# A 90-degree rotation on one core: stores on their own queue, issued when nearly all loads have landed

## Chip, cores, metric

One core of a Trainium2 chip. The metric is device time in microseconds (us), the median over executions. VectorE, ScalarE and SyncE are engines of the core; SBUF and PSUM are its on-chip memories; DMA engines move data between SBUF and the chip's main memory.

## The reference

```python
def setup_inputs():
    return {"x": np.random.randn(32, 3, 256, 256).astype(np.float32)}

def reference(x):
    return np.rot90(x, k=-1, axes=(-2, -1)).astype(np.float32)
```

25.17 MB go in and 25.17 MB come out. No arithmetic is done: data is loaded, transposed on VectorE in 32 x 32 blocks, and stored.

## The kernel before

The tensor is cut into 12 units of 2 MB, all of which fit into SBUF at once. Unit n is transposed into the buffer of unit n - 1, and the first unit into PSUM (`turned0`), from where ScalarE copies it at the end. No buffer has to be waited for, so the loads can run at full rate, and the stores follow in the same queue, SyncE's. A transfer of 1 MB is 128 packets of 8 KB (64 of 16 KB for most loads), and 16 DMA engines report its end.

```python
    for n in range(n_slabs):
        if n == last:
            nc.sync.dma_start(out=units[n], in_=ld8_v[n])          # 2 MB, 8 KB rows
            continue
        for i in range(I):
            if n == 0:
                nc.sync.dma_start(out=units[n][:, i], in_=ld8_v[n][:, i])
            else:                                                  # 1 MB, 16 KB rows
                nc.sync.dma_start(out=units[n][i::I].rearrange("p i f -> p (i f)"), in_=ld16_v[n, i])
    for n in range(n_slabs):
        t_in, t_out = units[n], units[n - 1] if n else turned0
        # ... two nc.vector.transpose from t_in to t_out (cut) ...
        if n == 1:
            nc.sync.dma_start(out=st_v[n][:, 0, :W], in_=t_out[:, 0, :W])   # 128 KB
            nc.sync.dma_start(out=st_v[n][:, 0, W:], in_=t_out[:, 0, W:])   # 896 KB
            nc.sync.dma_start(out=st_v[n][:, 1], in_=t_out[:, 1])           # 1 MB
        elif n:
            nc.sync.dma_start(out=st_v[n], in_=t_out)                       # 2 MB
    for i in range(I):
        nc.scalar.copy(out=units[last][:, i], in_=turned0[:, i])
    nc.sync.dma_start(out=st_v[0], in_=units[last])
```

Of the kernel before, what the change touches and what calls it, by code (L numbers as in the profile page):

```python
# [1 line left out]

# [4 lines left out]




@with_exitstack
def kernel(
    ctx: ExitStack,
    tc: tile.TileContext,
    x: bass.AP,
    out: bass.AP,
):

















    nc = tc.nc
    fp32 = mybir.dt.float32

    B, C, H, W = x.shape
    P = nc.NUM_PARTITIONS  # L40
    RI, RO = 16, 8
    K = H // RI
    I = 2
    Q = P // (K * I)
    n_slabs = B * C // (Q * I)
    last = n_slabs - 1
    F = RO * W

    rows_in = x.rearrange("b c h w -> (b c h) w")
    rows_out = out.rearrange("b c h w -> (b c h) w")  # L50
    ld8_v = rows_in.rearrange("(n i p r) w -> n p i (r w)", i=I, p=P, r=RO)
    ld16_v = rows_in.rearrange("(n i m r) w -> n i m (r w)", i=I, m=Q * K, r=RI)
    st_v = rows_out.rearrange("(n i p c) w -> n p i (c w)", i=I, p=P, c=RO)

    pools = [ctx.enter_context(tc.tile_pool(name=f"unit{u}", bufs=1)) for u in range(n_slabs)]
    units = [pool.tile([P, I, F], fp32, name=f"u{u}") for u, pool in enumerate(pools)]
    psum = ctx.enter_context(tc.tile_pool(name="psum", bufs=1, space=bass.MemoryType.PSUM))
    turned0 = psum.tile([P, I, F], fp32, name="turned0")

    for n in range(n_slabs):  # L60
        if n == last:
            nc.sync.dma_start(out=units[n], in_=ld8_v[n])
            continue
        for i in range(I):
            if n == 0:
                nc.sync.dma_start(out=units[n][:, i], in_=ld8_v[n][:, i])  # L66
            else:
                nc.sync.dma_start(out=units[n][i::I].rearrange("p i f -> p (i f)"), in_=ld16_v[n, i])

    for n in range(n_slabs):  # L70
        t_in, t_out = units[n], units[n - 1] if n else turned0
        if n in (0, last):
            for i in range(I):
                src = t_in[:, i].rearrange("p (r g c) -> p c r g", r=RO, c=RO)
                dst = t_out[:, i].rearrange("p (c g r) -> p c r g", c=RO, r=RO)
                nc.vector.transpose(out=dst[:, :, ::-1, ::-1], in_=src)  # L76
        else:
            src = t_in.rearrange("p i f -> p (i f)").rearrange("p (r g c) -> p c r g", r=RI, c=RO)
            dst = t_out.rearrange("p i (c k r) -> p c r k i", c=RO, r=RI)[:, :, ::-1, ::-1, :]
            for h in range(2):  # L80
                cs = slice(h * RO // 2, (h + 1) * RO // 2)
                nc.vector.transpose(out=dst[:, cs], in_=src[:, cs])  # L82

        if n == 1:
            nc.sync.dma_start(out=st_v[n][:, 0, :W], in_=t_out[:, 0, :W])
            nc.sync.dma_start(out=st_v[n][:, 0, W:], in_=t_out[:, 0, W:])
            nc.sync.dma_start(out=st_v[n][:, 1], in_=t_out[:, 1])
        elif n:
            nc.sync.dma_start(out=st_v[n], in_=t_out)  # L89

    for i in range(I):
        nc.scalar.copy(out=units[last][:, i], in_=turned0[:, i])  # L92
    nc.sync.dma_start(out=st_v[0], in_=units[last])


# [1 line left out]
_INS = ['x']  # L97
_OUTS = [((32, 3, 256, 256), 'float32')]


# [23 lines left out]
```

## Time and profile before

| | before |
|---|---|
| time | 124.06 us (3 runs) |
| span of the profile | 122.2 us |
| bytes over the span | 50.33 MB, 412 GB/s |
| rate inside loads and inside stores | 429 GB/s |
| "the turn" (last loads, first stores) | 59 to 63 us |

In the views below, a "stretch" line reads: start and end in us, length, busy time of VectorE, ScalarE and GpSimd, clock share, busy share of the DMA engines, GB/s. In a DMA view, the 40 numbers after `GB/s` are equal slices of the stretch asked for. Some statements rest on single packets: the trace records start and duration of each packet that a DMA engine moved, and of the 4-byte packet with which each of the 16 engines reports the end of a transfer. I call the time from the first to the last of these 16 reports of one transfer the *spread* of the engines. A transfer has landed when its semaphore, which counts these reports, is seen complete. Each profile is of one execution.

### The profile page before, as it was taken

The numbers are of one execution on the slowest core, as the hardware profiler recorded it, in microseconds if no ns is written. First come the engines' busy times: TensorE is split into PE (matmuls) and PEld (weight loads), VectorE is DVE, ScalarE is ACT, GpSimd is POOL, SyncE is SP. The second block draws the span as 40 slices with busy tenths as digits, with TensorE's granted clock in tenths as the row PEclk, the third lists the DMA queues.
The fourth block names the chain that finished last, engine by engine and source line by source line (L and its number), as shares of the span: only waits on it lengthen the run. The fifth ranks groups of instructions, "written<-read, shape, count | busy, mean of one in ns | idle before, by whom it ended". The sixth has DMA issues, their size and how long they took to land.

```text
span 122.2 us, 134 instructions
## 1 busy us (share of the span) xinstructions
DVE 93.3 (76%) x24; ACT 5.0 (4%) x3; POOL 0.2 (0%) x4
## 2 busy tenths in 40 slices
DVE  0299999999999999999999999999999940000000
ACT  0000000000000000000040000000000651000000
POOL 0000000000000000000000000000000000000000
DMA  3999999999999999999999999999999999999993
GB/s 88 429 432 434 440 440 429 429 429 429 429 429 429 429 429 424 434 424 408 370 414 428 426 429 429 429 429 429 429 429 429 424 429 429 429 429 426 429 429 166
DMA packets 5584, 50.33 MB, mean 412 GB/s; under 512 B 592, under 2 KB 720, under 8 KB 848
## 3 DMA queue, kind: packets, MB, share of 16 engines
q1 hardware_dynamic: 5584, 50.33, 97.8%
HBM read 25.17 MB, written 25.17 MB: 412 GB/s over the span
## 4 chain that ended last, share of the span: by engine, by line
DMA 57%; DVE 13%; issue 7%; DVEq 3%; ACT 2%; SPq 1%
DMA u<-in_x_dram 39%; DMA out_dram<-u 18%; DVE u L82 10%; DVE u L76 3%; DVEq L119 3%; ACT u L92 2%; SPq L66 1%; SPq L89 0%
## 5 line engine op out<-in xcount | busy, mean ns | idle before, releaser
L82 DVE STREAM_TRANSPOSE u<-u 128x2048 f32<-128x2048 f32 x20 | 78.0, 3948 | 0.3
L76 DVE STREAM_TRANSPOSE turned<-u 128x2048 f32<-128x2048 f32 x2 | 7.6, 3828 | 5.5 <-DMA u<-in_x_dram 5.5
L76 DVE STREAM_TRANSPOSE u<-u 128x2048 f32<-128x2048 f32 x2 | 7.8, 3953 | 0.0
L92 ACT COPY u<-turned 128x2048 f32<-128x2048 f32 x2 | 3.7, 1866 | 33.8 <-DVE u L76 33.8
L92 ACT ACT_TABLE_LOAD x1 | 1.3, 1283 | 62.4 <-DMA u<-in_x_dram 62.4
L108 POOL MEMSET const-bfloat16-1.0<- 128x1 bf16 x1 | 0.1, 102 | 0.0
L108 POOL MEMSET const-uint8-127<- 128x1 uint8 x1 | 0.1, 102 | 0.0
L108 POOL MEMSET const-float32-0.0<- 128x1 f32 x1 | 0.1, 99 | 0.2 <-issue 0.2
L108 POOL MEMSET const-float32-1.0<- 128x1 f32 x1 | 0.1, 99 | 0.0
## 6 DMA issues: line engine op xcount, KB each, us to landing
u<-in_x_dram SPq DMA_DIRECT2D x22, 1024.0 KB, 19.6
out_dram<-u SPq DMA_DIRECT2D x11, 2048.0 KB, 25.0
u<-in_x_dram SPq DMA_DIRECT2D x1, 2048.0 KB, 22.5
out_dram<-u SPq DMA_DIRECT2D x1, 1024.0 KB, 20.2
out_dram<-u SPq DMA_DIRECT2D x1, 896.0 KB, 20.2
out_dram<-u SPq DMA_DIRECT2D x1, 128.0 KB, 20.6
```

Source lines behind the costliest of these rows:

```text
L66: nc.sync.dma_start(out=units[n][:, i], in_=ld8_v[n][:, i])
L76: nc.vector.transpose(out=dst[:, :, ::-1, ::-1], in_=src)
L82: nc.vector.transpose(out=dst[:, cs], in_=src[:, cs])
L92: nc.scalar.copy(out=units[last][:, i], in_=turned0[:, i])
L108: nc = _bacc.Bacc("TRN2", target_bir_lowering=False, num_devices=1)
L119: with _tile.TileContext(nc) as tc:
```

## The change

The intent: keep loads and stores apart, each in a queue of its own, with transfers of mostly 1 MB. The first store waits until the first quarter of the last 1 MB has landed; the other three quarters are to cover the time that the store takes to start.

```diff
+    stores = []
+    def store(dst, src, after=None, cls=mybir.DependencyClass.NoSync):
+        st = nc.scalar.dma_start(out=dst, in_=src)
+        after = after or stores[-1]
+        tc.add_manual_dep(st.ins, after.ins.name, mybir.DependencyInfo(
+            cls, mybir.DependencyReason.SCHED_ONLY), reason="order of transfers")
+        stores.append(st)
     for n in range(n_slabs):
-        if n == last:
-            nc.sync.dma_start(out=units[n], in_=ld8_v[n])
-            continue
         for i in range(I):
-            if n == 0:
+            if n == last and i == 1:
+                parts = [slice(0, P, 4), slice(2, P, 4), slice(1, P, 2)]
+                lds = [nc.sync.dma_start(out=units[n][ps, i], in_=ld8_v[n][ps, i]) for ps in parts]
+            elif n in (0, last):
                 nc.sync.dma_start(out=units[n][:, i], in_=ld8_v[n][:, i])
         # ... cut ...
         if n == 1:
+            store(st_v[n][:, 0, :W], t_out[:, 0, :W], lds[0], mybir.DependencyClass.Sync)
+            store(st_v[n][:, 0, W:], t_out[:, 0, W:])
+            store(st_v[n][:, 1], t_out[:, 1])
+        elif n > last - 3:
+            store(st_v[n], t_out)
         elif n:
-            nc.sync.dma_start(out=st_v[n], in_=t_out)
+            for i in range(I):
+                store(st_v[n][:, i], t_out[:, i])
         # ... cut: the last 2 MB too are stored in two halves
```

More of the change, by code (lines that the diff above doesn't have):

```diff
@@ L84 @@
         if n == 1:
-            nc.sync.dma_start(out=st_v[n][:, 0, :W], in_=t_out[:, 0, :W])
-            nc.sync.dma_start(out=st_v[n][:, 0, W:], in_=t_out[:, 0, W:])
-            nc.sync.dma_start(out=st_v[n][:, 1], in_=t_out[:, 1])
+            store(st_v[n][:, 0, :W], t_out[:, 0, :W], lds[0], mybir.DependencyClass.Sync)
[3 more added lines that the diff above has]
+            store(st_v[n], t_out)
         elif n:
-            nc.sync.dma_start(out=st_v[n], in_=t_out)
+            for i in range(I):
+                store(st_v[n][:, i], t_out[:, i])
     for i in range(I):
         nc.scalar.copy(out=units[last][:, i], in_=turned0[:, i])
-    nc.sync.dma_start(out=st_v[0], in_=units[last])
+    for i in range(I):
+        store(st_v[0][:, i], units[last][:, i])
 _INS = ['x']
```

## The prediction

> **What bounds the kernel now.** I read the page first: busy table, slices, queue line, DMA issues. One queue carries everything, and the 16 DMA engines are busy for nearly the whole span.
>
> ```profile
> DVE 93.3 (76%) x24; ACT 5.0 (4%) x3; POOL 0.2 (0%) x4
> DMA  3999999999999999999999999999999999999993
> GB/s 88 429 432 434 440 440 429 429 429 429 429 429 429 429 429 424 434 424 408 370 414 428 426 429 429 429 429 429 429 429 429 424 429 429 429 429 426 429 429 166
> q1 hardware_dynamic: 5584, 50.33, 97.8%
> HBM read 25.17 MB, written 25.17 MB: 412 GB/s over the span
> ```
>
> The reader is to see three things. VectorE, at 76%, is not the bound. The rate stands at 429 GB/s in loads (first half) and in stores (second half) alike, so a store costs what a load costs. And there are only three places where the rate falls: the start, the slices 18 to 21 in the middle (408, 370, 414), and the end. 50.33 MB at 429 GB/s is 117.3 us of a span of 122.2 us; the whole change has 4.9 us to work on, and most of that is start and end.
>
> So I sized the three places. First the stretch where loads end and stores begin, as the table of chosen stretches has it (time, DVE, ACT, POOL, clock, DMA share, GB/s):
>
> ```profile
> 8.00:56.00 48.00, 47.79 (x13) 0.00 (x0) 0.00 (x0) 1.00 1.01 429
> 56.00:59.00 3.00, 3.00 (x2) 0.00 (x0) 0.00 (x0) 1.00 0.98 410
> 59.00:61.00 2.00, 1.97 (x2) 0.00 (x0) 0.00 (x0) 1.00 0.96 328
> 61.00:63.00 2.00, 2.00 (x1) 0.64 (x1) 0.00 (x0) 1.00 1.02 416
> 66.00:118.00 52.00, 33.09 (x9) 3.73 (x2) 0.00 (x0) 1.00 1.01 428
> ```
>
> Against 429 GB/s the turn loses 2.0 x (1 - 328/429) = 0.47 us, 3.0 x (1 - 410/429) = 0.13 us and 2.0 x (1 - 416/429) = 0.06 us: 0.66 us in all, with the engines still shown busy (0.96 to 1.02). They are not starved of work; packets take longer. The packet records say the same: 8 KB packets take 309 ns nearly everywhere, but 440 to 775 ns for the last few load packets of each engine between 59.3 and 60.8 us. By the packets that post each engine's share of a semaphore, the earliest engine loses 0.30 us there and the latest about 0.7 us, so the engines come out 0.6 us apart and stay so to the end.
>
> Then the start and the end, from the DMA view cut to 4 us (40 slices of 0.1 us):
>
> ```profile
> GB/s 0 0 0 0 0 0 0 0 0 0 0 0 0 0 0 0 0 410 246 0 164 0 0 0 492 164 0 573 328 246 573 410 328 492 492 328 492 492 328 492
> GB/s 246 573 410 328 573 410 328 573 410 328 492 410 328 492 492 246 410 655 246 246 246 328 82 164 0 0 0 0 0 0 0 0 0 0 0 0 0 0 0 0
> ```
>
> The first line is 0 to 4 us: data starts at 1.7 us and is at full rate from 2.4 us. The second is 118.2 to 122.2 us: the rate thins over the last 0.6 us (the engines that come in apart) and the last packet starts at about 120.5 us. Neither the first loads nor the last 2 MB are changed in kind.
>
> Last, who could be late for a store. The timeline:
>
> ```profile
> 0.73 0.86 SPq L66 DMA_DIRECT2D u<-in_x_dram  x2
> 42.28 0.36 SPq L85 DMA_DIRECT2D out_dram<-u  x1
> 49.60 50.02 SPq L89 DMA_DIRECT2D out_dram<-u  x10
> 91.47 7.75 DVE L76 STREAM_TRANSPOSE u<-u 128x2048 f32<-128x2048 f32 x2
> 99.26 1.87 ACT L92 COPY u<-turned 128x2048 f32<-128x2048 f32 x1 [1.93 <-DVE u L76]
> 101.15 0.37 SPq L93 DMA_DIRECT2D out_dram<-u  x1
> DMA to landing us min/median/max: 17.0/25.4/29.9
> ```
>
> The first store is issued at 42.28 us, 19 us before its turn: it stands in the ring behind the loads, so there is no gap at the turn. The last store is issued at 101.15 us and the last line (the view of the store line in the loop, L89) says that a store waits at least 17 us in the ring before it lands. VectorE's end at 99.2 us therefore has more than 10 us of slack.
>
> **What the Trainium skill says.** "DMA: Bandwidth & Descriptors", section "Issuing engines are not separate DMA queues", says that transfers started on different engines run on the same 16 DMA engines and interleave, and that issuing on several saves sequencer time alone. The trace before has one queue, so it can't show the interleaving, but issuing is not what it waits for. Same page, "Where 436 GB/s comes from": the fabric ceiling is 435 GB/s; the trace has 429, 98.6% of it, in both directions, so no faster stores are to be hoped for. Same page, "Latency and other measured facts": about 600 ns to the first byte for transfers issued from SyncE or ScalarE. The trace has about 1.0 us from the start of the first issue (0.73) to the first data (1.7), of which 0.39 us is the issuing instruction; I use 1.0 us. Same page, "Queues, rings and completion order": a DMA engine with work in two queues takes turns between them packet by packet, and a semaphore increment comes after that engine's earlier writes. In the trace the last store's semaphore packet ends at 120.83 us and it counts as landed at 121.18 us; over all transfers that step is 0.3 to 0.6 us, median 0.42 us.
>
> **The change part by part.**
>
> Stores move to ScalarE, their order pinned. Alone, this could let them run from 20 us on, among the loads; the wait on the first forbids it. Bytes are unchanged: 117.3 us stays.
>
> The last 1 MB load becomes 256 KB + 256 KB + 512 KB, every fourth partition, every fourth offset by two, every second. Each still spreads over the 16 engines (2, 2 and 4 packets of 8 KB on each), so an engine still has 8 x 306 ns = 2.45 us of work in it.
>
> The first store waits for the first 256 KB. When does that land? The semaphore packets of the last full 1 MB load of the row before are at 56.16 to 56.44 us (earliest and latest engine). The next 1 MB adds 2.45 us, to 58.89 us for the latest; two packets add 0.62 us, to 59.5; landing adds 0.42: 59.93 us. Other waits of that store (an earlier user of its semaphore, VectorE's third instruction) are long past. Issue and first data add 1.0 us: about 60.95 us. The remaining three quarters keep the engines busy until 56.16 + 2.45 + 2.45 = 61.06 us (earliest) to 61.34 us (latest). So the gap is about -0.1 to -0.4 us: the three quarters (768 KB, 1.83 us) just cover landing plus issue (1.42 us). If the first store's issue takes 0.4 us more than I think, a gap of at most 0.3 us opens. The first store is 128 KB in 1 KB rows, 46 ns a packet, 0.37 us an engine; the next follows about 0.43 us later, so at worst 0.06 us is lost between them.
>
> The store stream itself is not held up later. Eight semaphores are shared by loads and stores in turn, so about eight transfers of 1 MB can be under way, near 20 us of work. The store of the tenth 2 MB is issued at VectorE's 91.4 us and needed at about 61.3 + 18 x 2.45 = 105.4 us; the eleventh at 99.2 against 110. ScalarE must issue that one before its table load (1.28 us) and two copies (1.87 us each), so the last two 1 MB stores go out at about 102.5 and 104.4 us, needed at 115 and 117: slack of over 10 us. The sequencer's cost, 22 stores x about 0.37 us = 8 us, is spread over 40 us.
>
> Small change: 48 transfers in place of 37; 8 packets of 8 KB take 2.453 us with their semaphore packet and 2 MB take 4.900 us, so each extra transfer costs at most 5 ns of engine time, 0.05 us. At the end SyncE before first sat on the semaphore of the very last store and then checked three more pairs, 0.064 us each; now the last store's semaphore is checked last: -0.15 to -0.19 us.
>
> Sum: turn -0.66 us if the slow load packets were due to stores queued behind them, half of that as I don't know it; possible start-up of the new ring +0.15; extra transfers +0.05; end -0.17. -0.33 + 0.15 + 0.05 - 0.17 = -0.3 us, so 124.06 becomes about 123.8.
>
> **The rivals.**
>
> Gap at the turn. The new wait takes the place of a queue that ran ahead. For it: the margin I worked out is only 0.1 to 0.4 us, and the kernel's first packets took until 2.4 us to reach full rate, 0.7 us after the first data. Against: that ramp was a read from HBM with nothing under way, here engines still have loads. It would give 124.3 to 124.9.
>
> Full removal of the turn. If mixing queued stores with the last loads is the sole cause of the 440 to 775 ns packets, all of 0.66 us comes back, and the engines stay 0.3 us apart instead of 0.6: about 123.2 us. For it: the slow packets stop exactly where the stores start (309 ns again at 61 us). Against: the two queues still overlap for some packets in the new kernel, and the skill says they interleave.
>
> Slow stores from two queues or from ScalarE's ring. If stores of 1 MB ran below 429 GB/s, 25 MB would show it: 1% is 0.6 us. Against: 1 MB loads and 2 MB stores run at the same rate now. Over 125 us.
>
> Stores leaking in among loads, if the pinned order failed: the built order shows the wait on the first store and all others after it on ScalarE, so no.
>
> **Range and chances.** Prediction 123.8 us. The gains end at 123.1 (turn and end all won), the likely losses at 124.7 (a gap of 0.8 us and nothing won); I take these for 8 in 10. Faster by 2% is under 121.6, 2.5 us less, more than turn and end together hold: 2%. Slower by 2% is over 126.5, a gap of 2.5 us: more than landing plus issue can make in one place, 3%. Within 2%: 95%.
>
> **What would show it.** In slices of 0.2 us around 58 to 63 us: no zeros at the turn means the three quarters cover the issue; the stretch 59 to 61 us back at about 429 GB/s means that the queued stores slowed the last loads. The first ScalarE issue should stand at 59.7 to 60.1 us with first data 1.0 us later; the stores after it should hold 428; ScalarE's copies should stand after 99.3 us with nobody waiting. Wrong would be: a hole of over 0.5 us, a store phase below 425 GB/s, or a last issue later than 110 us.

## The result

The changed kernel takes **125.00 us** (124.95 to 125.08, 6 runs) against 123.99 us of before (123.74 to 124.13). The ratio is 1.0085, 95% interval 1.0072 to 1.0098. A ratio here is the mean time of one kernel's fast runs over that of the other's fast runs of the same rounds, so not quite the ratio of the medians. Within 2%, as said, but 1 us slower where 0.3 us faster was predicted, and outside the range of 123.1 to 124.7. All outputs are right.

The page of the changed kernel:

```profile
DMA  3999999999999999999999999999999999999995
GB/s 98 428 452 426 431 442 431 426 426 431 431 431 426 426 426 426 431 431 404 388 370 418 410 426 426 423 412 420 404 426 423 420 412 420 412 423 426 423 426 215
q10 hardware_dynamic: 3552, 25.17, 49.4%
q1 hardware_dynamic: 2208, 25.17, 48.4%
```

The loads (left half) are as before. The right half was an even 429 in the kernel before; now it wanders between 404 and 426 to the end, and the DMA engines are still shown as fully busy. This isn't a wait: the packets themselves take longer. The two queues carry 25.17 MB each.

Stretches of the changed kernel:

```profile
59.00:61.00 2.00, 1.97 (x2) 0.00 (x0) 0.00 (x0) 1.00 1.02 426
61.00:62.00 1.00, 1.00 (x1) 0.00 (x0) 0.00 (x0) 1.00 0.49 172
62.00:63.00 1.00, 1.00 (x1) 0.00 (x0) 0.00 (x0) 1.00 1.08 444
66.00:92.00 26.00, 25.86 (x8) 0.00 (x0) 0.00 (x0) 1.00 1.01 418
92.00:118.00 26.00, 7.23 (x2) 4.92 (x3) 0.00 (x0) 1.00 1.01 419
```

The same of the kernel before, as far as the prediction doesn't show them:

```profile
61.00:62.00 1.00, 1.00 (x1) 0.00 (x0) 0.00 (x0) 1.00 1.00 397
66.00:92.00 26.00, 25.86 (x8) 0.00 (x0) 0.00 (x0) 1.00 1.01 428
92.00:118.00 26.00, 7.22 (x2) 3.73 (x2) 0.00 (x0) 1.00 1.01 429
```

Three differences. The last loads run at 426 instead of 328 GB/s (59 to 61 us). Then the engines are idle for half of one microsecond (0.49 busy, 61 to 62 us). Then all stores run at 418 instead of 428 GB/s, over more than 50 us.

The timeline of the changed kernel, and the view of its store line from 60 to 62 us (min/median/max of the issuing instruction in ns):

```profile
60.17 39.47 ACTq L65 DMA_DIRECT2D out_dram<-u  x20
99.67 1.28 ACT L106 ACT_TABLE_LOAD   x1 [99.67 <-DMA out_dram<-u]
102.86 2.12 ACTq L65 DMA_DIRECT2D out_dram<-u  x2
L65 ACTq DMA_DIRECT2D out_dram<-u x3: 378/442/894, 60.2 to 61.6; - x3
```

The first store is issued at 60.17 us, and its first packet is at 61.08 us, 0.9 us later: as predicted. But the issuing instruction of the second store takes 894 ns, and its first packet comes at 62.05 us, 1.40 us after it began (60.65 us). That is 0.51 us after the end of the instruction (for the first store 0.53 us), so what came late is the instruction. By then the loads are done (last report at 61.50 us) and so is the first, small store (61.85 us). The table load and the copies at 99.67 us hold nobody up; the last store is issued at 104.6 us.

The account by the packet records, at the engine that comes last (an ordinary table, worked out from the reports and the spans):

| | before | changed | difference |
|---|---|---|---|
| all loads reported | 61.98 us | 61.50 us | -0.48 |
| from there to 1 MB stored | 2.49 us | 2.95 us | +0.46 |
| the other 23 MB | 56.36 us (2.450 a MB) | 57.58 us (2.503 a MB) | +1.22 |
| last report to end of span | 1.36 us | 1.15 us | -0.20 |
| span | 122.2 us | 123.2 us | +1.0 |

The gain among the loads and the loss at the first stores cancel. So what was to be found out is why a megabyte of stores went from 2.450 to 2.503 us.

### The profile page after: what moved, and what is told of

It reads as the page before. It is cut to its first block, busy times and chain, and to the rows that moved or that the text cites. A ratio compares the mean times of both kernels' runs of the same rounds, so it can differ in the third digit from the quotient of the medians.

```text
span 123.2 us, 147 instructions
## 1 busy us (share of the span) xinstructions
DVE 93.3 (76%) x24; ACT 4.9 (4%) x3; POOL 0.2 (0%) x4
## 3 DMA queue, kind: packets, MB, share of 16 engines
q10 hardware_dynamic: 3552, 25.17, 49.4%
q1 hardware_dynamic: 2208, 25.17, 48.4%
HBM read 25.17 MB, written 25.17 MB: 409 GB/s over the span
## 4 chain that ended last, share of the span: by engine, by line
DVE 33%; DMA 30%; issue 18%; ACT 3%; ACTq 0%
DMA out_dram<-u 26%; DVE u L93 26%; DVE turned L87 6%; DMA u<-in_x_dram 4%; ACT u L106 3%; ACT L106 0%; ACTq L65 0%
```

## The experiments

### Queue, or pause? Four runs

Two theories first. **Q**: ScalarE's queue is slower for stores. **S**: the pause at the turn lets all engines start again together, and this slows them down afterwards.

`e1`: the changed kernel, stores back on SyncE.

```diff
-        st = nc.scalar.dma_start(out=dst, in_=src)
+        st = nc.sync.dma_start(out=dst, in_=src)
```

> The changed kernel with its stores issued by SyncE again; wait, sizes and order stay. Two theories for the store phase that fell from 428 to 418 GB/s (2.45 to 2.50 us per MB). Theory Q: ScalarE's queue moves stores some 2% slower than SyncE's. It expects 426 to 429 GB/s between 66 and 118 us here, and a time near 124.0 us. Theory S: the pause of all 16 engines at the turn (61.5 to 62.05 us) lines the engines up, and lined-up engines run slower for the rest, whatever queue feeds them. It expects 416 to 421 GB/s and a time near 125.0 us, as the wait and its pause are kept.

Measured: 124.71 us, ratio 1.0045 (1.0033 to 1.0057).

`e3`: the kernel before with every `nc.sync.dma_start` made `nc.scalar.dma_start`.

> The kernel before with every transfer, loads too, issued by ScalarE: one queue, no wait added, no pause at the turn. Theory Q: the store phase is at 416 to 421 GB/s, the time 125.0 us or more (up to 126 if loads too are slower on this queue). Theory S: 426 to 429 GB/s and 124.0 us, as with the kernel before.

Measured: 124.22 us, ratio 1.0011 (0.9997 to 1.0025).

`e4`: the changed kernel with loads on `nc.scalar` and stores on `nc.sync`.

> The changed kernel with the queues swapped: loads by ScalarE, stores by SyncE, the wait kept. Theory Q: the store phase is at 426 to 429 GB/s; if the queue is slow for loads too, the loads from 8 to 56 us show 418 instead of 429. Theory S: the pause at the turn is still there and the store phase is at 416 to 421 GB/s, time near 125.0 us.

Measured: 125.05 us, ratio 1.0071 (1.0059 to 1.0083).

The store stretch of e1:

```profile
66.00:118.00 52.00, 33.15 (x9) 3.73 (x2) 0.00 (x0) 1.00 1.01 419
```

Of e3:

```profile
66.00:118.00 52.00, 33.12 (x9) 4.92 (x3) 0.00 (x0) 1.00 1.01 428
```

Of e4:

```profile
66.00:118.00 52.00, 33.36 (x9) 3.73 (x2) 0.00 (x0) 1.00 1.01 419
```

Theory Q is refuted from both sides: ScalarE's queue holds 428 GB/s when it carries the order of the kernel before, and SyncE's has 419 GB/s with that of the changed kernel. With e3's 124.22 us against 124.12 us of before, this agrees with the Trainium skill ("DMA: Bandwidth & Descriptors", section "Issuing engines are not separate DMA queues"): transfers run on the same 16 DMA engines whichever engine starts them.

But e1 did not keep the pause, as its expectation took for granted. With the stores on the loads' own queue the second store's instruction took 0.38 us instead of 0.89, and the DMA engines stayed busy. From 61 to 63 us e1 has:

```profile
61.00:63.00 2.00, 2.00 (x1) 0.00 (x0) 0.00 (x0) 1.00 1.00 399
```

The changed kernel has:

```profile
61.00:63.00 2.00, 2.00 (x1) 0.00 (x0) 0.00 (x0) 1.00 0.78 308
```

The 23 MB after the first took 57.48 us in e1 all the same (57.58 in the changed kernel). So the stores slowed down without the pause, and that theory S named e1's rate was luck.

`e2`: the changed kernel, but the wait is on the load before the three parts, so the stores come with 1 MB of loads still to go.

```diff
-            store(st_v[n][:, 0, :W], t_out[:, 0, :W], lds[0], mybir.DependencyClass.Sync)
+            store(st_v[n][:, 0, :W], t_out[:, 0, :W], ld_prev, mybir.DependencyClass.Sync)
```

> The changed kernel, but the first store waits for the load before the three parts (the first MB of the last unit), so 1 MB of loads is still to come when it is issued, and stores and loads overlap instead of pausing. Theory Q (slow ScalarE queue): the pause of about 0.5 us goes, the store phase stays at 416 to 421 GB/s, the time 124.5 to 125.0 us. Theory S (the pause lines the engines up): with no pause the store phase is at 426 to 429 GB/s and the time 123.5 to 124.1 us.

Measured: 124.19 us, ratio 1.0011 (0.9997 to 1.0025). Neither theory's time, and a profile that neither had:

```profile
66.00:74.00 8.00, 7.96 (x3) 0.00 (x0) 0.00 (x0) 1.00 1.01 428
74.00:82.00 8.00, 7.96 (x3) 0.00 (x0) 0.00 (x0) 1.00 1.01 426
82.00:92.00 10.00, 9.93 (x4) 0.00 (x0) 0.00 (x0) 1.00 1.01 420
92.00:118.00 26.00, 7.23 (x2) 4.92 (x3) 0.00 (x0) 1.00 1.01 420
```

The stores start at full rate and fall off while they run. By the packet records 97% of the 8 KB packets from 66 to 74 us take at most 311 ns, and 33% from 85 to 95 us. So here too a pause isn't necessary, and the stores can slow down while they run.

### Size of the stores? Four runs

Theory **P**: the packets of the 1 MB stores disturb each other; those of the 2 MB stores don't. (I supposed a certain division of the rows among the engines; no record shows it.)

`x1`: the changed kernel with the seven units stored as 2 MB again.

```diff
-            for i in range(I):
-                store(st_v[n][:, i], t_out[:, i])
+            store(st_v[n], t_out)
```

> The changed kernel with the stores of seven units as one transfer of 2 MB each again; queues, wait and load parts stay. The queue theory has fallen (ScalarE's queue held 428 GB/s with the stores of the kernel before, SyncE's had 419 with those of the changed kernel). Theory P (pattern): [...] packets of different engines get in each other's way (309 ns packets become 312 to 321). It expects 427 to 429 GB/s from 66 to 118 us here, and 124.0 to 124.2 us: the pause at the turn stays and costs little net. Theory S (the pause lines up the engines) expects 416 to 421 GB/s and 125.0 us.

Measured: 125.15 us, ratio 1.0087 (1.0073 to 1.0101).

`x2`: the kernel before with these seven units stored in halves.

```diff
-        elif n:
+        elif n > last - 3:
             nc.sync.dma_start(out=st_v[n], in_=t_out)
+        elif n:
+            for i in range(I):
+                nc.sync.dma_start(out=st_v[n][:, i], in_=t_out[:, i])
```

> The kernel before with its stores of seven units in halves of 1 MB, nothing else changed: SyncE alone, no wait, no pause. Theory P expects jittering packets and 416 to 424 GB/s from 66 to 118 us (perhaps starting late, as in the run with the earlier wait), and 124.5 to 125.1 us. Theory S expects 428 GB/s, no packet over 311 ns, and 124.1 us.

Measured: 124.09 us, ratio 1.0005 (0.9993 to 1.0018). The store stretch of x1:

```profile
66.00:118.00 52.00, 33.12 (x9) 4.92 (x3) 0.00 (x0) 1.00 1.01 419
```

Of x2:

```profile
66.00:118.00 52.00, 33.18 (x9) 3.73 (x2) 0.00 (x0) 1.00 1.01 428
```

Size and pattern make no difference in either kernel. Theory P, which I had thought likely, is refuted.

`x3`: e2 with 2 MB stores (the diffs of e2 and x1 together).

> The changed kernel with both: the first store waits for the load before the three parts, and the stores of seven units are of 2 MB. This should be the best of all if theory P is right: no pause at the turn, 428 GB/s to the end, 123.5 to 123.8 us. Theory S also expects no slow phase here. If 2 MB stores jitter too once two queues have been mixed at the turn, it stays at 124.2 us or over.

Measured: 124.29 us, ratio 1.0018 (1.0005 to 1.0032), not the best of all: its packets become uneven from about 66 us on, and from 66 to 118 us it has 421 GB/s.

`x4`: the kernel before with only its last load cut like that of the changed kernel.

```diff
-        if n == last:
-            nc.sync.dma_start(out=units[n], in_=ld8_v[n])
-            continue
         for i in range(I):
-            if n == 0:
+            if n == last and i == 1:
+                for ps in (slice(0, P, 4), slice(2, P, 4), slice(1, P, 2)):
+                    nc.sync.dma_start(out=units[n][ps, i], in_=ld8_v[n][ps, i])
+            elif n in (0, last):
```

> The kernel before with only its last load cut like that of the changed kernel (1 MB, then 256, 256 and 512 KB): no wait, one queue, 2 MB stores. If the slow load packets before the turn (328 GB/s from 59 to 61 us) come from stores that stand behind the loads in the same ring, they stay: 320 to 380 GB/s there and 124.0 to 124.2 us. If they come from the 2 MB shape of the last load, they go: 420 GB/s or more there and about 123.5 us. Store phase 428 GB/s in either case.

Measured: **123.82 us**, ratio 0.9981 (0.9969 to 0.9994), the only version here that beats the kernel before, by 0.2%.

```profile
59.00:61.00 2.00, 1.97 (x2) 1.28 (x1) 0.00 (x0) 1.00 0.99 397
61.00:63.00 2.00, 2.00 (x1) 0.00 (x0) 0.00 (x0) 1.00 0.98 392
66.00:92.00 26.00, 25.86 (x8) 0.00 (x0) 0.00 (x0) 1.00 1.01 428
```

397 GB/s at the turn lies between the two values expected, so what slows the last loads isn't decided by it. Its last packet ends at 120.68 us, 0.14 us before that of the kernel before, and from the last landing to the end of the span it takes 0.8 instead of 1.0 us: its last store uses a semaphore that SyncE checks last.

### A pause put where none was

`t4`: the kernel before; in the middle of its stores, one waits for the one before it to land. Later stores keep their order.

```diff
+            st = nc.sync.dma_start(out=st_v[n], in_=t_out)
+            if n > 4:
+                cls = mybir.DependencyClass.Sync if n == 5 else mybir.DependencyClass.NoSync
+                tc.add_manual_dep(st.ins, held.ins.name, mybir.DependencyInfo(
+                    cls, mybir.DependencyReason.SCHED_ONLY), reason="pause")
+            held = st
```

> The kernel before with a pause in the middle of its stores: the store of the fifth unit written back is issued only when that of the fourth has landed (about 81.4 us), so all engines run dry for about 1.4 us and start again together. One queue, 2 MB stores, the turn untouched. So far neither queue nor store size explains the slow store phase; what the slow runs share is that the engines' last semaphore packets of a transfer come within 0.15 to 0.55 us of each other, in the fast runs 0.6 to 0.8 us. Theory T (spread): engines that run closely together disturb each other, engines that are two packets (0.61 us) or more apart do not. It expects 428 GB/s from 66 to 80 us, a spread under 0.3 us after the pause and 416 to 421 GB/s from 84 to 118 us; time 124.1 + 1.4 + 0.8 = about 126.3 us. If spread does not matter, 428 GB/s after the pause too and about 125.5 us.

Measured: 126.47 us, ratio 1.0207 (1.0192 to 1.0222); whether that is slower by 2% is unclear.

```profile
66.00:80.00 14.00, 13.93 (x5) 0.00 (x0) 0.00 (x0) 1.00 1.01 428
81.00:83.00 2.00, 2.00 (x1) 0.00 (x0) 0.00 (x0) 1.00 0.22 90
84.00:100.00 16.00, 15.12 (x4) 2.68 (x2) 0.00 (x0) 1.00 1.01 417
100.00:118.00 18.00, 0.00 (x0) 1.05 (x1) 0.00 (x0) 1.00 1.01 419
```

This run shows that a pause is enough. One queue, one transfer size, one execution: 428 GB/s before the pause, 417 to 419 after it, for the remaining 34 us. The spread is 0.61 us before and 0.19 us after. Before the pause every 8 KB packet takes at most 311 ns (median 309); after it, from 85 to 95 us, 65% take longer (mean of all 317). e1 shows that a pause isn't needed.

### Is it the spread?

Theory **T**: engines that run closely together disturb each other; two packets (0.61 us) apart they don't. `t1` takes the changed kernel and puts one extra load among its stores, meant to hold back 8 engines only; `t2` is its control with 16 rows; `t3` has loads of 8, 4, 2 and 1 rows.

```diff
+        if n == 4:
+            store(pad[0:8, :3840], ld16_v[0, 0][:8, :3840])        # t1
+            store(pad[0:16, :1920], ld16_v[0, 0][:16, :1920])      # t2 in place of it
+            # t3: 8, 4, 2 and 1 rows of 2048 at partitions 0, 32, 64, 96
```

> The changed kernel with one extra load of 8 rows of 15 KB into an unused tile, put among the stores after the fourth unit (about 81.6 us). It should run on 8 of the 16 engines alone and hold those back by 0.57 us. Theory T expects 418 GB/s from 66 to 80 us, a spread of about 0.75 us after it, and 427 to 429 GB/s from 84 to 118 us; the time about 125.0 - 0.7 + 0.57 = 124.9 us at most, as the held engines also end later. If spread does not matter: 418 GB/s throughout and 125.5 us.

> Control: the same 123 KB extra load, but as 16 rows, so that all 16 engines are held back by the same 0.29 us. Theory T expects no change of spread, 416 to 421 GB/s from 84 to 118 us and 125.3 us.

> The changed kernel with four extra loads of 8 KB rows at the same place, of 8, 4, 2 and 1 rows: if these go to the lowest 8, 4, 2 and 1 engines, the engines come to stand in five groups 0.31 us apart, 1.2 us from first to last. Theory T expects 427 to 429 GB/s from 84 to 118 us, as with one extra load or better; a time of 125.0 to 125.5 us, as one engine ends 1.2 us late.

Measured: t1 126.17 us (ratio 1.0186, 1.0169 to 1.0203), t2 125.29 us (1.0114, 1.0099 to 1.0130), t3 127.57 us (1.0297, 1.0281 to 1.0312). The rates of t1 before and after its extra load:

```profile
66.00:80.00 14.00, 13.93 (x5) 0.00 (x0) 0.00 (x0) 1.00 1.02 421
84.00:100.00 16.00, 15.19 (x4) 0.34 (x1) 0.00 (x0) 1.00 1.01 422
```

Of t2:

```profile
66.00:80.00 14.00, 13.93 (x5) 0.00 (x0) 0.00 (x0) 1.00 1.01 420
85.00:97.00 12.00, 11.96 (x4) 0.00 (x0) 0.00 (x0) 1.00 1.01 427
100.00:118.00 18.00, 0.00 (x0) 4.44 (x3) 0.00 (x0) 1.00 1.01 425
```

t1 and t3 miss: a spread of over 1 us between two or more groups (t3: 421 GB/s from 84 to 118 us) doesn't bring 428 back. In t1 from 85 to 95 us 57% of the packets were at most 311 ns. Nor was t1 the test it was meant to be: by the reports its load held 8 engines back by some 1.5 us, not 0.57 (its 15 KB packets took 793 to 941 ns), and left two groups of 8, each within 0.3 us. In t3 the engines' last reports lie 2.5 us apart, from 121.93 to 124.41 us. The control t2, where I expected nothing, went the other way: its small load held the engines back unequally, the spread went from 0.18 to 0.60 us, 99% of the packets were at most 311 ns from 85 to 95 us, and later the rate fell again: packets became uneven (5% from 95 to 100 us) while the spread still stood at 0.60 us, and by 117 us it had shrunk to 0.26 us. That its time was the one expected was luck. So theory T is wrong as I put it, in terms of first and last engine. That how the engines stand to each other matters is a reading of t2 and t4, not shown by itself; the one number "spread" is at best a rough measure of it.

### Lateness, or two queues? Three more runs

`f1`: e2 with the stores on SyncE (diffs of e1 and e2). `f2` and `f3`: the changed kernel, the first store waiting for the last load of the unit before the last, and of the one before that, so that 2 and 4 MB of loads are still to go.

> The changed kernel with the wait on the load before the three parts and the stores on SyncE's queue again: one ring, stores issued about 59.5 us with 1 MB of loads still to come. If mixing two queues is what keeps the engines close (0.52 us), one ring gives a spread of 0.6 us or more as in the kernel before, no packet jitter, 427 to 429 GB/s from 66 to 118 us and 123.7 to 124.0 us. If the late issue is what matters, the spread is under 0.55 us, the rate falls to 418 to 424 GB/s and the time is 124.2 to 124.8 us.

> The changed kernel with its two queues, the first store waiting for the last load but 2 MB: loads and stores mixed for about 4 MB. If the spread at the end of the mixing decides, longer mixing should give more of it: over 0.6 us, 427 GB/s or more and 123.6 to 123.9 us. If mixing two queues always leaves the engines close, 418 to 424 GB/s and 124.2 us or more.

> As the run before it, with 4 MB of loads to come: about 8 MB mixed. Same reading: over 0.6 us of spread and 427 GB/s or more, 123.5 to 123.9 us, if mixing spreads the engines; 124.2 us or more, with 418 to 424 GB/s, if it does not. If mixed traffic itself is slow, 56 to 70 us shows under 420 GB/s and the time is 124.5 us or more.

Measured: f1 124.56 us, ratio 1.0047 (1.0029 to 1.0064); f2 124.20 us, 1.0015 (0.9995 to 1.0035); f3 124.03 us, 1.0002 (0.9989 to 1.0015). The store stretch of f1 falls off like that of e2 with one queue only, so two queues aren't the cause:

```profile
66.00:118.00 52.00, 33.07 (x9) 3.73 (x2) 0.00 (x0) 1.00 1.01 422
```

The turn and the store stretch of f2:

```profile
59.00:61.00 2.00, 1.97 (x2) 0.00 (x0) 0.00 (x0) 1.00 0.93 349
66.00:118.00 52.00, 33.19 (x9) 4.92 (x3) 0.00 (x0) 1.00 1.01 427
```

The store stretch of f3:

```profile
66.00:118.00 52.00, 33.37 (x9) 4.92 (x3) 0.00 (x0) 1.00 1.01 427
```

f2 and f3 issue their stores later than the kernel before too, on the second queue, and hold 427 GB/s. The changed kernel, e2, f2 and f3 differ in one thing alone, the load that the first store waits for: with 768 KB of loads to go the stores run at 418 GB/s, with 1 MB at 422, with 2 MB and with 4 MB at 427. So a late start does matter, but only when less than 2 MB of loads are left. f2 pays at the turn (349 GB/s) and its engines end 1.57 us apart, so it gains nothing (its profiled execution is the slowest of six, 124.67 us). Not one of the two-queue versions beat the kernel before.

All runs whose engines ran without a later disturbance, from the packet records (spread: median over the transfers reported from 66 to 74 us; clean: share of 8 KB packets of at most 311 ns, from 66 to 74 and from 85 to 95 us):

```
run      queue of stores  MB a store  spread us  clean 66-74  clean 85-95
before   SyncE            2           0.61       100%         100%
e3       ScalarE          2           0.70       100%         100%
x4       SyncE            2           0.67       100%         100%
x2       SyncE            1           0.83       100%          99%
f3       ScalarE          1           1.07        99%         100%
f2       ScalarE          1           1.57       100%          99%
x3       ScalarE          2           0.53        84%          21%
e2       ScalarE          1           0.52        97%          33%
f1       SyncE            1           0.44        97%          22%
e1       SyncE            1           0.29        37%          15%
e4       SyncE            1           0.17        35%          16%
changed  ScalarE          1           0.15        37%          13%
x1       ScalarE          2           0.15        27%          13%
```

The runs fall into three groups by spread: from 0.6 us up clean to the end, 0.44 to 0.53 us mostly clean at first and then decaying, under 0.3 us slow at once. Inside a group the order isn't strict. Queue and size are mixed through the groups. But the wait sorts the runs in the same way: no wait or 2 MB and more to go, 1 MB to go, 768 KB to go. So the table can't tell the spread from the wait, and the spread isn't a rule: in f1 it grew to 0.71 us by 111 us, while only 9% of the packets from 105 to 118 us were clean.

## Why the prediction was wrong, by its own steps

- **"The store stream itself is not held up later": this step failed.** It looked for late issues, of which there were none; it took for granted that stores once running run at 428 GB/s "at the same rate now" as before. The 23 MB after the first cost 1.22 us more, all of the loss and more. The rival "slow stores from two queues or from ScalarE's ring" had the size (it counted 0.6 us for 1%; the fall from 428 to 418 is 2.3%) and the wrong mechanism, as e1, e3 and e4 show. What the runs showed in its place: the wait itself sets the rate of the stores after it, 418 GB/s with 768 KB of loads to go and 427 with 2 MB (f2). Packets of 8 KB go from 309 ns to a mean of 315 (66 to 118 us). A pause alone does the same, for the rest of the execution (t4); e1 has it without one. What happens between the engines stays open.
- **The turn**: the first part was right. Landing was foreseen at 59.93 us and was at 60.07 us; first data at 60.95 us and came at 61.08 us; end of loads 61.06 to 61.34 us, and it was 60.97 to 61.50 us. The mis-sized term is the next store: "the next follows about 0.43 us later, so at worst 0.06 us is lost". Its issuing instruction took 0.89 us and its data came 1.40 us after it began. In the stretch from 61 to 62 us the engines were idle for half of the time. Why this second issue is slow no run here shows: it took 0.86 us in e4 and 0.93 in x1, but 0.38 in e1, on the loads' queue, and 0.39 in e2, on a queue of its own. The sum for the sequencer, "22 stores x about 0.37 us = 8 us", was too low as well: the instructions took 338 to 1287 ns, 17.8 us in all. After the turn this held nobody up.
- **The gain at the turn** was half right. The last loads gained 0.48 us, between the 0.33 us that the sum counted and the 0.66 us at most; 0.46 us of it was lost again by the end of the first MB of stores, with the pause. The stated reason, that stores queued behind them slow the loads, isn't shown: f2, with its stores in the other queue, has the dip as well.
- **The end**: -0.17 us predicted, -0.20 us measured. **ScalarE's copies and VectorE's slack**: as predicted, with the last store issued at 104.6 us.
- **The range** summed a pause of up to 0.8 us "and nothing won", but had no term for what happens to the stores afterwards. Of its own signs of being wrong, "a store phase below 425 GB/s" is the one that came true; the hole was about 0.5 us.

One more thing can be read from the records: the disorder at the turn that costs the kernel before some 0.7 us also drives its engines apart (from 0.27 to 0.61 us). The changed kernel, e2 and f1 lose less among the last loads, start their stores closer together, and pay later. That one is the price of the other is a reading, not shown.

What stays open: why stores run slower after a late start or a pause, and whether it is that engines disturb each other when they write closely together. The records don't tell the engine of a packet. That the late start is the cause rests on the changed kernel, e2, f2 and f3, which differ in the wait alone; that a pause can be one, on t4. For the spread there is only company: the grouping of 13 single executions, t2 and t4 for it, f1 and the end of t2 against it.

## What to carry to other kernels

In a kernel bound by transfers, be wary of a wait that holds the first stores back until the loads have nearly run out, whether or not the DMA engines then run dry: here what the loads gained (0.48 us) was lost at once, and the slower stores cost 1.2 us more. When a wait is moved, look not only for idle time but compare the rate in the phase after it with that of the kernel before; fully busy DMA engines can be 2.3% slower. Issue stores early, behind the loads of the same queue, if nothing speaks against it; cutting only the last load, as in x4, was the only gain found here (0.2%).

## What the Trainium skill lacked or had wrong

- "DMA: Bandwidth & Descriptors" (no section has it): how the stores start sets their rate for long after. 8 KB packets took 309 ns in the kernel before and a mean of 315 ns where the stores started with 768 KB of loads to go, 428 against 418 GB/s; in t4 one pause turned 428 into 417 to 419 GB/s for the rest of the execution.
- The same page, "Latency and other measured facts", has about 600 ns to the first byte for SyncE and ScalarE. That fits when it is counted from the end of the issuing instruction (0.62 us at the kernel's start, 0.53 for the first store, 0.51 for the second). What it lacks is that the instruction itself took 338 to 1287 ns for the same 1 MB store.
- No page has that the last loads before the stores slow down (8 KB packets of 440 to 775 ns at the turn of the kernel before, 328 GB/s from 59 to 61 us); the runs don't settle why.
